# A SwiGLU FFN in two phases: gate and up of the latent tokens as seven half-size products each, the activations kept in DRAM between

## The chip, the core and the metric

One core of one Trainium2 chip runs the whole program. The metric is the device time of one execution in microseconds (us); the kernel before was run three times, and the median counts. Engines are named as the profile names them: PE (TensorE, matmuls; PEld is its weight load), DVE (VectorE), ACT (ScalarE), POOL (GpSimd) and SP (SyncE, whose queue issues the DMAs).

## The reference, cut to what matters

Two layers. Each has a token mixer and then an FFN on 1280 tokens of 1024 channels: 256 context tokens and 1024 latent ones. The mixer ends in a dense output projection `w_out`. The FFN of a layer is

```python
def _swiglu(h, w_gate, w_up, w_down):
    return (jax.nn.silu(h @ w_gate) * (h @ w_up)) @ w_down

FFN_HIDDEN = -(-8 * D_MODEL // (3 * 256)) * 256      # 2816
```

on `h`, the residual stream after an RMS norm, a gain and a shift. Its result is normalised and added to the residual stream. All inputs and weights are float32.

## The kernel before, in words

**Layout.** Activations are channel-major, `[128, 8 channel tiles, tokens]`, and the tokens form three blocks `BLK`: block 0 is the 256 context tokens, blocks 1 and 2 are 512 latent tokens each. Layer 1 is the last one and drops the context (only blocks 1 and 2 go through its FFN).

**Precision.** Every dense product is three matmuls in float32r. A weight is split into a rounded part and the rest: a cast on ACT (`whi`, line 433) and a subtraction on POOL (`wlo`, line 434), in `weights`. An activation is split the same way into `xh` and `xl`. `dense_cm` (line 440) then runs, for each of eight tiles of 128 input channels, whi.xh, whi.xl and wlo.xh into one PSUM bank: 24 matmuls for 128 output channels of one block.

**The FFN** (`out_ffn`, line 1455) runs passes over the blocks: block 1, then blocks 0 and 2 together (layer 0), or block 1, then block 2 (layer 1). A pass goes through 11 pairs `pr` of hidden tiles of 128. For each hidden tile of the pair it loads and splits the 128 columns of gate and of up, runs `dense_cm` for both, takes the silu from exponentials and a logarithm (`silu`, line 727), multiplies (line 1490), and splits the product into `hh` (ACT, line 1491) and `hl` (DVE, line 1492). Then, in the same iteration, it multiplies with the pair's rows of `w_down`, split into `dh` (ACT, line 1502) and `dl` (POOL, line 1503), and adds the result on DVE (line 1517) into `facc`, or copies it there on ACT for the first pair (line 1515). So a pair costs one block 96 matmuls for gate and up and 48 for down, and nothing of the hidden activations leaves the chip.

**Around it.** `w_out` (line 1441) projects the mixers' outputs, which `y_load` (line 1428) reads back from DRAM (`yt`) and splits; blocks 1 and 0 are projected while the GLA mixer, the last of the three, still runs, block 2 after it. `mid` in `run` is `resid` (line 388: RMS norm of the projection, gain, add to the residual stream loaded from DRAM, store) followed by `split_norm` (line 374: the second norm, into `xh` and `xl`). `rstd` (line 345) is the sum of squares: ACT squares, DVE and POOL add (lines 366, 368). `out_ffn` emits two of block 2's eight output tiles of `w_out`, then `mid(1)`, the other six, `mid(0)` and `mid(2)`, and then the passes.

**What sets the order.** The Tile framework orders each engine's instructions when the program is built: it takes the order in which the code emits them as priority, and lets a later instruction that its own simulated timeline shows ready go ahead. At run time every queue is in order, SP's too. PSUM is eight banks of 512 float32 a partition: three for `pd` (gate, up, projections), three for `pm` (down), two for `pn` (norms).

## Time and profile before

| | us |
|---|---|
| median of three runs (4211.9 to 4219.88) | 4216.71 |
| the profiled execution, span from first to last instruction | 4221.6 |
| PE busy in it | 3927.3 |
| the stretch of layer 0's FFN | about 1240 to 2250 |
| the stretch of layer 1's FFN, to the end | 3377 to 4222 |

The profiled execution has no time of its own beside its span; the span lies 4.9 us above the median of the runs. A matmul's duration in a row is longer than the step from one matmul to the next, because matmuls are pipelined: the step is read from start to start. A group of rows gives the count, the busy time, the mean duration of one in nanoseconds, and the idle time before them with what ended it. Some matmul records are missing from the trace, so counts of matmuls are taken from the code.

### The profile page before, as it was taken

Reading aid. Unit: us, or ns where it says so; the run is one execution under the profiler, and the core shown is the slowest. Engines: PE = TensorE matmul, PEld = TensorE weight load, DVE = VectorE, ACT = ScalarE, POOL = GpSimd, SP = SyncE. Lnnn points to the kernel's source line nnn. Section 1 sums busy time; section 2 is a strip of 40 time slices with the busy share of each in tenths; the row PEclk is TensorE's granted clock in tenths of the full one; section 3 lists DMA queues with packets and bytes.
Section 4 is the critical chain, followed back from the end, with each engine's and each line's share of the span. In section 5 each row is a group of like instructions: output and inputs, shape, how many; then the busy total and the mean of one; then the engine's idle time right before and its main releaser. Section 6 shows DMA issues by size and latency. Waiting matters only on the chain. (4 is left out here: it accounts for less than half of the span.)

```text
span 4221.6 us, 74050 instructions
## 1 busy us (share of the span) xinstructions
PE 3927.3 (93%) x29094; PEld 3157.3 (75%) x29094; DVE 2346.4 (56%) x4053; ACT 1629.1 (39%) x3267; POOL 1730.6 (41%) x1686
## 2 busy tenths in 40 slices
PE   7998999899999999999998997999888979999998
PEld 3776888776677788888885675887856757888886
DVE  4565656658756633644445464666658565335444
ACT  4442334234435333522224443343244344334332
POOL 3155630323456544522223145640423465445443
PEclk8998999899999999999998998999989989999999
DMA  6586545665433333322222387554764253334332
GB/s 191 129 235 183 140 125 146 191 186 184 126 120 112 108 92 106 97 65 60 61 60 92 86 225 202 129 148 135 206 196 122 66 157 96 99 94 134 93 97 93
DMA packets 822655, 547.18 MB, mean 130 GB/s; under 512 B 317853, under 2 KB 727201, under 8 KB 822305
## 3 DMA queue, kind: packets, MB, share of 16 engines
q1 hardware_dynamic: 822016, 541.38, 44.9%
q8 instruction: 229, 3.75, 0.4%
q14 instruction: 122, 0.99, 0.1%
q0 software_dynamic: 288, 1.05, 0.1%
HBM read 421.96 MB, written 120.33 MB: 128 GB/s over the span
## 5 line engine op out<-in xcount | busy, mean ns | idle before, releaser
L243 PE MATMUL pd<-xh,whi 128*128 128x512 f32 (+1 forms) x2608 | 981.8, 377 | 30.8 <-ACT whi L433 13.9
L434 POOL TENSOR_TENSOR wlo<-wraw,whi 128x1024 fp32r<-128x1024 f32 (+1 forms) x328 | 678.4, 2072 | 786.8 <-ACT whi L433 652.2
L243 PE MATMUL pd<-xl,whi 128*128 128x512 f32 (+1 forms) x2608 | 987.7, 379 | 12.4 <-DVE xl L1437 4.6
L243 PE MATMUL pd<-xh,wlo 128*128 128x512 f32 (+1 forms) x2608 | 982.5, 377 | 15.7 <-POOL wlo L434 15.7
L243 PEld LDWEIGHTS pd<-xh,whi 128*128 128x128 f32 x2608 | 500.3, 192 | 135.1 <-DVE xh L384 18.8
L243 PEld LDWEIGHTS pd<-xl,whi 128*128 128x128 f32 x2608 | 500.5, 192 | 122.9 <-issue 13.4
L243 PEld LDWEIGHTS pd<-xh,wlo 128*128 128x128 f32 x2608 | 500.6, 192 | 118.3 <-POOL wlo L434 20.5
L433 ACT CAST whi<-wraw 128x1024 fp32r<-128x1024 f32 (+1 forms) x328 | 289.2, 891 | 483.1 <-PE pd L243 266.9
L1517 DVE TENSOR_TENSOR f<-pm,f 128x512 f32<-128x512 f32 (+1 forms) x400 | 247.2, 635 | 354.1 <-PE pm L243 354.1
L1503 POOL TENSOR_TENSOR dl<-draw,dh 128x512 fp32r<-128x512 f32 x176 | 242.6, 1378 | 480.2 <-ACT dh L1502 450.8
L243 PE MATMUL pm<-hl,dh 128*128 128x512 f32 (+1 forms) x880 | 327.6, 373 | 8.1 <-DVE hl L1492 8.1
L243 PE MATMUL pm<-hh,dh 128*128 128x512 f32 (+1 forms) x880 | 322.3, 374 | 9.4 <-DVE f L1517 3.9
L243 PE MATMUL pd<-whi,xh 128*128 128x256 f32 x1072 | 317.6, 297 | 1.9 <-DVE st L438 1.9
L243 PE MATMUL pm<-hh,dl 128*128 128x512 f32 (+1 forms) x880 | 318.2, 372 | 0.0
L243 PE MATMUL pd<-wlo,xh 128*128 128x256 f32 x1072 | 317.8, 297 | 0.0
L243 PE MATMUL pd<-whi,xl 128*128 128x256 f32 x1072 | 317.7, 297 | 0.0
L1502 ACT CAST dh<-draw 128x512 fp32r<-128x512 f32 x176 | 109.1, 620 | 456.7 <-DMA draw<-in_w_ffn_down 245.1
L236 ACT ACTIVATE silu<-silu 128x512 f32<-128x512 f32 (+2 forms) x332 | 171.7, 517 | 191.9 <-DVE silu L731 185.7
L243 PEld LDWEIGHTS pd<-whi,xh 128*128 128x128 f32 x1072 | 213.2, 199 | 8.9 <-issue 3.2
L243 PEld LDWEIGHTS pd<-wlo,xh 128*128 128x128 f32 x1072 | 214.1, 200 | 7.1 <-issue 5.4
L243 PEld LDWEIGHTS pd<-whi,xl 128*128 128x128 f32 x1072 | 213.5, 199 | 7.2 <-issue 5.0
L1492 DVE TENSOR_TENSOR hl<-sg,hh 128x512 fp32r<-128x512 f32 (+1 forms) x110 | 179.5, 1632 | 57.1 <-ACT hh L1491 57.1
(296 smaller groups left out, 7161.2 us busy)
## 6 DMA issues: line engine op xcount, KB each, us to landing
wmod<-in_w_mod SPq DMA_DIRECT2D x192, 256.0 KB
draw<-in_w_ffn_down SPq DMA_DIRECT2D x176, 256.0 KB
wraw<-in_w_ffn_gate SPq DMA_DIRECT2D x88, 512.0 KB
wraw<-in_w_ffn_up SPq DMA_DIRECT2D x88, 512.0 KB
wraw<-in_w_in SPq DMA_DIRECT2D x100, 256.0 KB
a<-ops SPq DMA_DIRECT2D x80, 288.0 KB
X<-ops SPq DMA_DIRECT2D x36, 480.0 KB
wraw<-in_w_out SPq DMA_DIRECT2D x32, 512.0 KB
```

Source lines behind the costliest of these rows:

```text
L236: i = self.nc.scalar.activation(out, in_, f, bias=bias, scale=scale)
L243: return self.nc.tensor.matmul(out, l, r, start=start, stop=stop)
L433: nc.scalar.copy(wh[i][:, :, w], r)
L434: nc.gpsimd.tensor_tensor(wl[i][:, :, w], r, wh[i][:, :, w].bitcast(F32), op=ALU.subtract)
L1492: nc.vector.tensor_tensor(hl[q][b], sg, hh[q][b].bitcast(F32), op=ALU.subtract)
L1502: nc.scalar.copy(dh[:, w], raw)
L1503: nc.gpsimd.tensor_tensor(dl[:, w], raw, dh[:, w].bitcast(F32), op=ALU.subtract)
L1517: nc.vector.tensor_tensor(facc[b][:, m, :], ps[:, :n], facc[b][:, m, :], op=ALU.add)
```

## The change

The FFN becomes `ffn`, in two phases.

**Phase 1** makes the hidden activations and stores them in DRAM (`self.H`). For latent tokens the 2x2 block form of the product, two halves of the 1024 input channels by two hidden tiles by two halves of the tokens, takes seven products of half size in place of eight (`quad`; Strassen's scheme in Winograd's variant). The sums of activations are made once for each layer (`operands`, `operands_late`), the sums of weights for every quad on DVE (`diff`), and the sums of products when PSUM is read. Two of the products accumulate onto a bank that has been read (`first=False`). Layer 0 takes block 1 and block 2 as the two halves (512 columns a matmul) and does the context block alone before that, with plain products (`hidden_plain`). Layer 1 halves each block (256 columns a matmul): the first two pairs (`J1`) for block 1 alone, pairs 2 to 10 for both blocks with shared weights, then the first two for block 2. `gate` takes the silu of a whole pair at once.

**Phase 2** loads the activations again, splits them (`hh`, `hl`) and does the down product, in the passes of before.

Beside that: gate, up, down and output weights are laid out by the host so that one load is `[128, 2048]` with a partition's 8 KB in one run; they are split in pieces of 512 columns (`slot`, four in flight); `w_out` yields after two output tiles instead of one. `pd` has four banks in the FFN and `pn` one. The norms' scratch `nv` has two buffers instead of four. The second norm is made in place (`norm_here`) before the operands, and the residual loads go to a pool of their own (`XO`). Pools for norms, projections and FFN move to other places in SBUF; between the layers the PSUM pools are closed and opened again. The mixers are as before.

The core of the diff (the removed `out_ffn` and `w_out` are in the listing above; `res`, `norm` are `resid`, `norm_here` of block b; what follows the down product is as before):

```diff
-NV = 4
+NV = 2
...
+NS = 4
+J1 = 2
...
+        self.H = [self.t(self.dram, [128, HT, TOK], f"h{i}") for i in range(2)]
...
+    def norm_here(self, x, b, A, B, s):
+        n = BLK[b][1]
+        rs = self.t(self.N, [128, 512], "nrs", bufs=1)[:, :n]
+        self.rstd(x, b, rs)
+        for kt in range(KT):
+            (self.nc.gpsimd if kt % 3 == 2 else self.nc.vector).tensor_tensor(x[:, kt, :], x[:, kt, :], rs, op=ALU.mult)
+            self.act(x[:, kt, :], x[:, kt, :], AF.Identity, bias=B[:, kt, s:s + 1], scale=A[:, kt, s:s + 1])
+    def resid(self, f, b, gp, s, xsrc, xdst, pe=False, px=None):
-        xo = self.t(self.A2 if b == 2 else self.A01, [128, KT, n], f"xl{b}")
...
         self.dma(xo, xsrc[:, :, t0:t0 + n])
         rs = self.t(self.N, [128, 512], "nrs", bufs=1)[:, :n]
...
+    def raw(self, p, src):
+        r = self.t(p, [128, 2048], "raw", bufs=2)
+        self.dma(r, src)
+        return r
+    def slot(self, p, src, e):
+        hi = self.t(p, [128, 512], "shi", F32R, bufs=NS)
+        lo = self.t(p, [128, 512], "slo", F32R, bufs=NS)
+        self.nc.scalar.copy(hi, src)
+        e.tensor_tensor(lo, src, hi.bitcast(F32), op=ALU.subtract)
+        return hi, lo
+    def mm3(self, ps, w, c0, xh, xl, start, stop, skip=False):
+        a, c = w[0][:, c0:c0 + 128], w[1][:, c0:c0 + 128]
+        self.mm(ps, a, xh, start, False, skip)
+        self.mm(ps, a, xl, False, False, skip)
+        self.mm(ps, c, xh, False, stop, skip)
+    def w_out(self, l, p, bs, f, bank, py):
+        y = {b: self.y_load(l, b, f[b], py) for b in bs}
+        for m2 in range(KT // 2):
+            raw = self.raw(p, self.I["wo"][l, m2])
+            for m in range(2):
+                w = [self.slot(p, raw[:, 1024 * m + 512 * k:1024 * m + 512 * k + 512], self.nc.gpsimd) for k in range(2)]
+                for b in bs:
+                    ps = bank()[:, :BLK[b][1]]
+                    for kt in range(KT):
+                        self.mm3(ps, w[kt // 4], 128 * (kt % 4), y[b][0][:, kt, :], y[b][1][:, kt, :], kt == 0, kt == KT - 1)
+                    self.nc.scalar.copy(f[b][:, 2 * m2 + m, :], ps)
             yield
...
+    PRODUCTS = ("11", "S2", "S3", "S1", "12", "22", "S4")
+    def operands(self, xc, p, T):
+        nc = self.nc
+        v, g = nc.vector, nc.gpsimd
+        n = xc["11"][0].shape[2]
+        def split(name, kt, src, e):
+            h, lo = xc[name]
+            nc.scalar.copy(h[:, kt, :], src)
+            e.tensor_tensor(lo[:, kt, :], src, h[:, kt, :].bitcast(F32), op=ALU.subtract)
+        for kt in range(4):
+            split("11", kt, T[0][:, kt, :], g if kt % 2 else v)
+        for kt in range(4):
+            a11, a12, a21, a22 = T[0][:, kt, :], T[0][:, kt + 4, :], T[1][:, kt, :], T[1][:, kt + 4, :]
+            s1, s2, s3 = (self.t(self.N, [128, 512], x, bufs=1)[:, :n] for x in ("nsq", "nacc", "nacc2"))
+            v.tensor_tensor(s1, a21, a22, op=ALU.add)
+            v.tensor_tensor(s2, s1, a11, op=ALU.subtract)
+            v.tensor_tensor(s3, a11, a21, op=ALU.subtract)
+            v.tensor_tensor(a21, a12, s2, op=ALU.subtract)
+            for i, (name, src) in enumerate((("S2", s2), ("S3", s3), ("S1", s1), ("12", a12))):
+                split(name, kt, src, g if i % 3 == 2 else v)
+    def operands_late(self, xc, T):
+        for i, name in enumerate(("22", "S4")):
+            h, lo = xc[name]
+            for kt in range(4):
+                x = T[1][:, kt + 4 - 4 * i, :]
+                self.nc.scalar.copy(h[:, kt, :], x)
+                self.nc.vector.tensor_tensor(lo[:, kt, :], x, h[:, kt, :].bitcast(F32), op=ALU.subtract)
+    def xc_tiles(self, p, names, n, i):
+        return {x: tuple(self.t(p, [128, 4, n], f"{x}{k}{i}", F32R) for k in "hl") for x in names}
+    def quad(self, W, S, raw, xcs, out):
+        nc = self.nc
+        v, g = nc.vector, nc.gpsimd
+        ng, n = len(xcs), xcs[0]["11"][0].shape[2]
+        B = raw.rearrange("p (k c x) -> p k c x", k=2, c=2)
+        o = out.rearrange("p c (g t x) -> p c t g x", g=ng, t=2)
+        def diff(a, b):
+            t = self.t(W, [128, 512], "tw", bufs=3)
+            v.tensor_tensor(t, a, b, op=ALU.subtract)
+            return t
+        def prod(bank, name, src, e, first=True):
+            w = self.slot(W, src, e)
+            for i, xc in enumerate(xcs):
+                h, lo = xc[name]
+                for kt in range(4):
+                    self.mm3(bank[:, i * n:i * n + n], w, 128 * kt, h[:, kt, :], lo[:, kt, :],
+                             first and i == 0 and kt == 0, i == ng - 1 and kt == 3, not first)
+        def u(tag):
+            return self.t(S, [128, ng * n], tag, bufs=2)
+        def r(x):
+            return x.rearrange("p (g x) -> p g x", g=ng)
+        pa, pb, pc, pd = (self.pd()[:, :ng * n] for _ in range(4))
+        prod(pa, "11", B[:, 0, 0], g)
+        s1 = u("s1")
+        nc.scalar.copy(s1, pa)
+        t1 = diff(B[:, 0, 1], B[:, 0, 0])
+        t2 = diff(B[:, 1, 1], t1)
+        prod(pb, "S2", t2, v)
+        u2 = u("u2")
+        v.tensor_tensor(u2, pb, s1, op=ALU.add)
+        t3 = diff(B[:, 1, 1], B[:, 0, 1])
+        prod(pc, "S3", t3, v)
+        u3 = u("u3")
+        v.tensor_tensor(u3, pc, u2, op=ALU.add)
+        prod(pd, "S1", t1, v)
+        v.tensor_tensor(o[:, 1, 1], r(pd), r(u3), op=ALU.add)
+        prod(pa, "12", B[:, 1, 0], g, False)
+        nc.scalar.copy(o[:, 0, 0], r(pa))
+        t4 = diff(B[:, 1, 0], t2)
+        prod(pc, "22", t4, v, False)
+        v.tensor_tensor(o[:, 0, 1], r(pc), r(u2), op=ALU.add)
+        prod(pd, "S4", B[:, 1, 1], g, False)
+        v.tensor_tensor(o[:, 1, 0], r(pd), r(u2), op=ALU.add)
+    def gate(self, S, g, n):
+        nc = self.nc
+        e = self.t(S, [128, 2, n], "e")
+        nc.vector.tensor_scalar(e, g, -80.0, None, op0=ALU.max)
+        self.act(e, e, AF.Exp, scale=-1.0)
+        self.act(e, e, AF.Ln, bias="one")
+        self.act(e, e, AF.Exp, scale=-1.0)
...
+    def hidden(self, l, W, S, j, xcs, t0):
+        n = len(xcs) * 2 * xcs[0]["11"][0].shape[2]
+        o = []
+        for i in range(2):
+            raw = self.raw(W, self.I["wgu"][l, j, i])
+            x = self.t(S, [128, 2, n], "gu"[i])
+            self.quad(W, S, raw, xcs, x)
+            if i == 0:
+                self.gate(S, x, n)
+            o.append(x)
+        self.nc.vector.tensor_tensor(o[1], o[1], o[0], op=ALU.mult)
+        self.dma(self.H[l][:, 2 * j:2 * j + 2, t0:t0 + n], o[1])
+    def hidden_plain(self, l, W, S, j, xh, xl, b):
+        nc = self.nc
+        t0, n = BLK[b]
+        g = self.t(S, [128, 2, n], "g0")
+        h = self.t(S, [128, 2, n], "u0")
+        for i in range(2):
+            raw = self.raw(W, self.I["wgu"][l, j, i])
+            for c in range(2):
+                ps = self.pd()[:, :n]
+                for k in range(2):
+                    w = self.slot(W, raw[:, 1024 * k + 512 * c:1024 * k + 512 * c + 512], nc.gpsimd)
+                    for kt in range(4):
+                        self.mm3(ps, w, 128 * kt, xh[:, 4 * k + kt, :], xl[:, 4 * k + kt, :], k == 0 and kt == 0, k == 1 and kt == 3)
+                if i == 0:
+                    nc.scalar.copy(g[:, c, :], ps)
+                else:
+                    nc.vector.tensor_tensor(h[:, c, :], ps, g[:, c, :], op=ALU.mult)
+            if i == 0:
+                self.gate(S, g, n)
+        self.dma(self.H[l][:, 2 * j:2 * j + 2, t0:t0 + n], h)
...
+            for g in gs:
+                g.__exit__(None, None, None)
+        if not last:
+            gXO, XO = self.pool("XO", side=self.a)
+            next(wo)
+            res(0, XO)
+            for _ in wo:
+                pass
+            over(gY)
+            res(1, XO)
+            res(2, XO)
+            over(gXO)
+            gX, X = self.pool("XC", side=self.a)
+            xc = self.xc_tiles(X, self.PRODUCTS[:5], 512, 0)
+            g0, p0 = self.pool("X0", side=self.a)
+            norm(0)
+            xh0, xl0 = (self.t(p0, [128, KT, 256], x, F32R) for x in ("xh0", "xl0"))
+            for kt in range(KT):
+                nc.vector.tensor_copy(xh0[:, kt, :], f[0][:, kt, :])
+                nc.gpsimd.tensor_tensor(xl0[:, kt, :], f[0][:, kt, :], xh0[:, kt, :].bitcast(F32), op=ALU.subtract)
+            T = [f[1], f[2]]
+            for j in range(HT // 2):
+                self.hidden_plain(l, W, p0, j, xh0, xl0, 0)
+                if j == 1:
+                    norm(1)
+                if j == 3:
+                    norm(2)
+                if j == 6:
+                    self.operands(xc, X, T)
+            over(g0)
+            gX1, X1 = self.pool("XC1", side=self.a)
+            xc.update(self.xc_tiles(X1, self.PRODUCTS[5:], 512, 0))
+            self.operands_late(xc, T)
+            over(self.gF2, self.gF01, self.gN)
+            gS, S = self.pool("S", side=self.o)
+            for j in range(HT // 2):
+                self.hidden(l, W, S, j, [xc], 256)
+            over(gS, gX1, gX)
+        else:
+            gX, X = {}, {}
+            xc = []
+            for b in (1, 2):
+                gXO, XO = self.pool("XO", side=self.a)
+                if b == 1:
+                    next(wo)
+                res(b, XO)
+                over(gXO)
+                norm(b)
+                gX[b], X[b] = self.pool("XC", side=self.a)
+                xc.append(self.xc_tiles(X[b], self.PRODUCTS, 256, b))
+                T = [f[b][:, :, 256 * k:256 * k + 256] for k in range(2)]
+                self.operands(xc[-1], X[b], T)
+                self.operands_late(xc[-1], T)
+                if b == 1:
+                    for _ in wo:
+                        pass
+                    over(gY, self.gF01)
+                    gS, S = self.pool("S", side=self.o)
+                    for j in range(J1):
+                        self.hidden(l, W, S, j, xc[:1], 256)
+            over(gS, self.gF2, self.gN)
+            gS, S = self.pool("S", side=self.o)
+            for j in range(J1, HT // 2):
+                self.hidden(l, W, S, j, xc, 256)
+            for j in range(J1):
+                self.hidden(l, W, S, j, xc[1:], 768)
+            over(gS, gX[2], gX[1])
...
+        self.gN, self.N = self.pool("N", side=self.a)
+        for bs in [(1,), (2,) if last else (0, 2)]:
             facc = {b: self.f_tiles(self.F2 if b == 2 else self.F01, [b])[b] for b in bs}
             for pr in range(HT // 2):
+                raw = self.raw(W, I["wd"][l, pr])
                 hh, hl = {}, {}
...
+                    t0, n = BLK[b]
+                    h = self.t(Dp, [128, 2, 512], "h")[:, :, :n]
+                    self.dma(h, self.H[l][:, 2 * pr:2 * pr + 2, t0:t0 + n])
+                    k, bufs = (0, 1) if b == 0 else (1, 2)
+                    hh[b] = self.t(Dp, [128, 2, n], f"hh{k}", F32R, bufs=bufs)
+                    hl[b] = self.t(Dp, [128, 2, n], f"hl{k}", F32R, bufs=bufs)
+                    nc.scalar.copy(hh[b], h)
+                    nc.vector.tensor_tensor(hl[b], h, hh[b].bitcast(F32), op=ALU.subtract)
+                for half in range(2):
+                    w = [self.slot(W, raw[:, 1024 * q + 512 * half:1024 * q + 512 * half + 512], nc.gpsimd) for q in range(2)]
+                    for m4 in range(4):
+                        m = 4 * half + m4
+                        for b in bs:
+                            n = BLK[b][1]
+                            ps = self.pm()[:, :n]
+                            for q in range(2):
+                                self.mm3(ps, w[q], 128 * m4, hh[b][:, q, :], hl[b][:, q, :], q == 0, q == 1)
+                            if pr == 0:
+                                nc.scalar.copy(facc[b][:, m, :], ps)
+                            else:
+                                nc.vector.tensor_tensor(facc[b][:, m, :], ps, facc[b][:, m, :], op=ALU.add)
```

## Rows read from the trace of the kernel before

**Rows 1.** The page's first part: busy time, share of the span, instructions, by engine.

```profile
PE 3927.3 (93%) x29094; PEld 3157.3 (75%) x29094; DVE 2346.4 (56%) x4053; ACT 1629.1 (39%) x3267; POOL 1730.6 (41%) x1686
```

**Rows 2.** Stretches of the two layers' FFNs: busy by engine, granted clock, DMA.

```profile
core 0: us, PE busy (x) PEld busy (x) DVE busy (x) ACT busy (x) POOL busy (x), PEclk, DMA share, GB/s
1300.00:1700.00 400.00, 383.32 (x1637) 307.86 (x1638) 208.23 (x257) 159.95 (x243) 203.97 (x117) 0.98 0.35 106
1700.00:2200.00 500.00, 495.75 (x2835) 432.43 (x2834) 226.79 (x339) 170.35 (x280) 171.73 (x94) 0.99 0.23 68
3377.00:3540.00 163.00, 132.32 (x525) 102.32 (x525) 110.49 (x103) 79.03 (x120) 107.30 (x57) 0.90 0.44 135
3540.00:4180.00 640.00, 639.10 (x2784) 523.10 (x2783) 271.06 (x320) 227.88 (x326) 294.86 (x159) 1.00 0.34 101
4180.00:4222.00 42.00, 22.26 (x80) 14.46 (x78) 18.93 (x25) 9.41 (x15) 6.04 (x4) 0.83 0.30 107
```

**Rows 3.** Chain that ended last, one period of the second layer: start, us, what.

```profile
3588.72 4.59 PE pd L243 x20
...
3621.74 4.59 PE pd L243 x20
```

**Rows 4.** Timeline of ACT, layer 0, second pass: one cast, a period apart.

```profile
2172.95 0.61 ACT L1491 CAST hh<-sg 128x512 fp32r<-128x512 f32 x1
...
2223.04 0.61 ACT L1491 CAST hh<-sg 128x512 fp32r<-128x512 f32 x1
```

**Rows 5.** Timeline of PE: 256-column matmuls back to back, 15 steps apart.

```profile
2174.09 0.28 PE L243 MATMUL pd<-xl,whi 128*128 128x256 f32 x1
...
2175.79 0.28 PE L243 MATMUL pd<-xl,whi 128*128 128x256 f32 x1
```

**Rows 6.** Groups of POOL by shape: count, busy us, mean ns.

```profile
L434 POOL TENSOR_TENSOR wlo<-wraw,whi 128x1024 fp32r<-128x1024 f32 x208 | 509.0, 2448 | 406.1 <-ACT whi L433 297.3 <-PE pd L243 100.5 <-PE pg L243 4.8
L1503 POOL TENSOR_TENSOR dl<-draw,dh 128x512 fp32r<-128x512 f32 x176 | 242.6, 1378 | 480.2 <-ACT dh L1502 450.8 <-PE pd L243 16.2 <-PE pm L243 11.0
...
L386 POOL TENSOR_TENSOR xl<-nv,xh 128x512 fp32r<-128x512 f32 x32 | 47.9, 1503 | 40.1 <-DVE xh L384 40.1
...
L398 POOL TENSOR_TENSOR nv<-f,nrs 128x512 f32<-128x512 f32 x16 | 28.5, 1780 | 40.8 <-ACT nrs L236 23.2 <-DVE f L399 17.6
```

**Rows 7.** Groups of DVE by shape: count, busy us, mean ns.

```profile
L1517 DVE TENSOR_TENSOR f<-pm,f 128x512 f32<-128x512 f32 x320 | 215.3, 689 | 333.7 <-PE pm L243 333.7
L1492 DVE TENSOR_TENSOR hl<-sg,hh 128x512 fp32r<-128x512 f32 x88 | 168.5, 1914 | 47.6 <-ACT hh L1491 47.6
...
L735 DVE TENSOR_TENSOR sg<-pd,silu 128x512 f32<-128x512 f32 x88 | 60.8, 691 | 176.3 <-ACT silu L236 176.2
...
L1492 DVE TENSOR_TENSOR hl<-sg,hh 128x256 fp32r<-128x256 f32 x22 | 11.0, 500 | 9.5 <-ACT hh L1491 9.5
```

**Rows 8.** Timeline of DVE, layer 1: the same subtraction, short and long.

```profile
3399.87 0.68 DVE L1437 TENSOR_TENSOR xl<-f,xh 128x512 fp32r<-128x512 f32 x1
...
3401.13 1.76 DVE L1437 TENSOR_TENSOR xl<-f,xh 128x512 fp32r<-128x512 f32 x1
```

**Rows 9.** Groups of ACT by shape: count, busy us, mean ns.

```profile
L1502 ACT CAST dh<-draw 128x512 fp32r<-128x512 f32 x176 | 109.1, 620 | 456.7 <-DMA draw<-in_w_ffn_down 245.1 <-PE pm L243 211.0
...
L236 ACT ACTIVATE nsq<-f 128x512 f32<-128x512 f32 x81 | 50.9, 628 | 71.8 <-DVE nacc L366 35.2 <-POOL nacc L368 13.6 <-DVE f L1517 9.7
```

**Rows 10.** Timelines of SP and ACT: when layer 1's loads of yt are issued, land.

```profile
3377.65 2.39 SPq L246 DMA_DIRECT2D f<-yt  x3
```

**Rows 11.** Instructions that touch f: copies of block 2's output projection, last start.

```profile
L1449 ACT COPY f<-pd x16: 567/576/585, 1259.5 to 3456.0; 128x512 f32<-128x512 f32 x16
...
3384.38 1.66 ACT L1436 CAST xh<-f 128x512 fp32r<-128x512 f32 x3 [0.32 <-DMA f<-yt]
```

**Rows 12.** Timeline of DVE, layer 1: block 2's residual and norm.

```profile
3468.54 4.79 DVE L398 TENSOR_TENSOR nv<-f,nrs 128x512 f32<-128x512 f32 x3 [0.74 <-ACT nrs L236]
...
3520.91 0.79 DVE L384 CAST xh<-nv 128x512 fp32r<-128x512 f32 x2
```

More of the change, by code (lines that the diff above doesn't have):

```diff
@@ L196, in pd @@
     def pd(self):
-        return self.psd.tile([128, 512], F32, tag="d", name=self.nm("pd"), bufs=3)
+        return self.psd.tile([128, 512], F32, tag="d", name=self.nm("pd"), bufs=self.nd)
     def pm(self):
@@ L202, in pn @@
     def pn(self):
-        return (self.psr if self.banks[2] == NB1 else self.psum).tile([128, 512], F32, tag="n", name=self.nm("pn"), bufs=self.banks[2])
+        return (self.psum if self.banks[1] else self.psr).tile([128, 512], F32, tag="n", name=self.nm("pn"), bufs=self.banks[2])
     def pt(self, tag, bufs):
@@ L240, in act, with mm @@
         return i
-    def mm(self, out, l, r, start=True, stop=True):
-        return self.nc.tensor.matmul(out, l, r, start=start, stop=stop)
+    def mm(self, out, l, r, start=True, stop=True, skip=False):
+        return self.nc.tensor.matmul(out, l, r, start=start, stop=stop, skip_group_check=skip)
     def dma(self, out, in_):
@@ L1439, in y_load @@
         return yh, yl
-    def w_out(self, l, p, bs, f, bank):
-        y = {b: self.y_load(l, b, f[b]) for b in bs}
-        for m in range(KT):
-            w = self.weights(p, [(0, self.I["w_out"][l][:, 128 * m:128 * m + 128])], 128)
-            for b in bs:
-                ps = bank()[:, :BLK[b][1]]
-                self.dense_cm(ps, *w, *y[b])
-                self.nc.scalar.copy(f[b][:, m, :], ps)
+    def raw(self, p, src):
[24 more added lines that the diff above has]
+                    self.nc.scalar.copy(f[b][:, 2 * m2 + m, :], ps)
             yield
@@ L1453, in f_tiles @@
         return {b: self.t(p, [128, KT, BLK[b][1]], f"f{b}") for b in bs}
-    def out_ffn(self, l, passes, f, mid, xh, xl, gp2, A1n, B1n):
-        nc, I = self.nc, self.I
-        self.gF2, self.F2 = self.pool("F2", side=self.a)
-        gW, W = self.pool("W3", side=self.a)
-        last = l == DEPTH - 1
-        f.update(self.f_tiles(self.F2, [2]))
-        wo = self.w_out(l, W, [2], f, self.pd)
-        for _ in range(WM):
-            next(wo)
-        if WM:
-            mid(1)
-        for _ in wo:
-            pass
-        for b in passes[1][::MO]:
-            mid(b)
+    PRODUCTS = ("11", "S2", "S3", "S1", "12", "22", "S4")
@@ new lines, in ffn, with res, norm, over @@
+    def ffn(self, l, f, gp1, A2, B2, gp2, A1n, B1n):
+        nc, I = self.nc, self.I
+        last = l == DEPTH - 1
+        xsrc = self.XD[0] if l else I["xt"]
+        gW, W = self.pool("W", side=self.a)
+        gY, Y = self.pool("Y", side=self.o)
+        wo = self.w_out(l, W, [2], f, self.pd, Y)
+        def res(b, px):
+            self.resid(f[b], b, gp1, 1 if b == 0 else 0, xsrc, self.XD[1], px=px)
+        def norm(b):
+            self.norm_here(f[b], b, A2, B2, 1 if b == 0 else 0)
+        def over(*gs):
+            for g in gs:
[65 more added lines that the diff above has]
+            over(gS, gX[2], gX[1])
+        self.gA01, self.A01 = self.pool("A01", side=self.o)
+        self.gA2, self.A2 = self.pool("A2", side=self.o)
+        self.gF01, self.F01 = self.pool("F01", side=self.a)
+        self.gF2, self.F2 = self.pool("F2", side=self.a)
+        self.gN, self.N = self.pool("N", side=self.a)
+        gD, Dp = self.pool("D", side=self.a)
```

105 lines of the change are left out of this document (34 added, 71 removed).

## The prediction

> **What bounds the kernel now.** I read the page's busy shares first, then the FFNs by stretch, then the chain that ended last for the step of a matmul, then single operations. PE is busy 93% of the span and no other engine over 56% [rows 1]. A matmul's record overlaps the next one's, so the stretches say more: in the settled part of layer 1's FFN PE idles 0.9 of 640 us, in layer 0's 4.3 of 500, at a granted clock of 1.00 and 0.99 [rows 2]. There PE's stream of instructions is the bound, and a matmul that goes is worth its step. At the starts it isn't: PE idles 30.7 of 163 us in layer 1 (clock 0.90) and 16.7 of 400 in layer 0 [rows 2], where projection, residual, norm and split follow one another. The change shortens the settled parts and rebuilds the starts.
>
> **The unit.** A pair of hidden tiles is 144 matmuls of 512 columns for a block. The chain repeats after 33.02 us [rows 3], 0.2293 us each. With the context in the pass, 144 of 256 columns join them and the period is 50.09 us [rows 4]: 17.07/144 = 0.1185 us for 256 columns. Back to back such a step is 0.1133 us [rows 5].
>
> **What the products save.** Layer 0: gate and up of both latent blocks go from 192 to 168 matmuls a pair, 24 x 0.2293 = 5.50 us, in 11 pairs 60.5. Layer 1 halves the columns as well: 192 x 0.2293 = 44.03 us become 336 x 0.1185 = 39.82, in 11 pairs 46.3. At 0.1133 it would be 65.5. I take 0.1185, which a whole pass gave, and keep the other end. The context's gate and up and all down products keep their matmuls; they only move.
>
> **Does a quad stay PE's?** A quad (gate or up of a pair) is 84 x 0.2293 = 19.3 us of PE. POOL has three subtractions at 1.378 us, 4.1 [rows 6]. DVE has five reads of PSUM at 0.69 [rows 7], eight operations with both inputs in SBUF (four weight sums, four subtractions), and its half of gate and last multiplication, six units of 512 columns, four of them with two SBUF inputs. Such an operation takes 0.68 us, or 1.76 [rows 8], and 1.91 on the mean for `hl` at L1492 [rows 7]. With 0.68 DVE needs 13 us a quad; with 1.91 it needs 3.5 + 15.3 + 9.0 = 27.8 and would be the bound. L1492 ran while POOL was busy 294.86 of 640 us [rows 2], mostly in instructions of 2.45 us [rows 6]; in a quad POOL is busy 21% in pieces of 1.38. Scaling the excess of 1.23 us by 21/46 and by 1.38/2.45 gives 0.32: 1.0 us each, 17 us of DVE a quad. So PE leads, by 2.3 us. ACT, with seven casts and two copies at 0.62 and six units of gate at 0.63 [rows 9], has 9.4. PSUM leaves two products or more between a read and the bank's next use, 5.5 us, and four slots of weights three products. So in the settled part I price the new DVE, ACT and POOL work at nothing, hidden under PE; what it costs without that cover is the second rival.
>
> The Trainium skill (SBUF — State Buffer, Who interferes with whom) says that a DVE instruction with two SBUF inputs and a POOL instruction that reads SBUF exclude each other, the later one blocked until the first has ended, and that DVE reading PSUM isn't touched. The trace agrees: 1.91 us at L1492, 0.69 at L735. By the rule such an operation waits for at most one POOL subtraction, on the mean 0.21 x 0.69 = 0.14 us as an estimate, and DVE would need 15 us; the sum stays, the rival gets weaker.
>
> **Layer 0's context stage** is new on its own: 1056 matmuls x 0.1185 = 125.1 us of PE. Its weights used to be shared with block 2 under PE; now POOL splits them for 256 columns alone. POOL: 88 subtractions x 1.378 = 121.3; the context's own 8, half as wide, 6; two norms (each three additions at 1.378 and two multiplications at 1.78), 15.4; six splits of operands at 1.50, 9.0 [rows 6]. That is 152 us: POOL becomes the bound and 27 us are lost. Ends: 0, where PE's 125 cover all, and 62, with every operation at 1.78. Each of its 22 loads is 1 MB through two buffers. In layer 1 the first 1.25 MB of `yt` landed 6.7 us after the issue [rows 10]; with 6 us for 1 MB the buffers turn in (6 + 5.5)/2 = 5.8 us against POOL's 5.5, at worst 6 us in all. In return the 16.7 us of idle in this stretch go, as I count all of its time anew.
>
> **Between the phases** the first loads need pairs stored long ago. Stores of 1 MB a pair have 38 us each; SP waits for the last multiplication of a pair with the next loads queued behind it, but these are two quads ahead. A pair of the down product is 48 x 0.2293 = 11 us of PE; its activations need load, cast and subtraction, some 8 us through one buffer, and are ready. I take 4 us a layer for the switch, 8; ends 0 and 27, if the first load must wait for the last store (6.7 us each way, twice).
>
> **Smaller scratch** (`nv`) lengthens residuals and norms where PE waits: kernel start, between the layers, the tail of 42 us [rows 2]. I take 5 us, ends 0 and 12.
>
> **Layer 1's start.** Block 2's projection ended at 3456.6 [rows 11], its norm and split at 3521.7 [rows 12]: 65 us. That was covered by the first pass of block 1. Now only four quads of block 1 at 256 columns may run, 4 x 84 x 0.1185 = 39.8 us. Behind the projection come residual and norm (65 less some 8 for the split) and then 16 sums and 22 subtractions at 0.50 [rows 7], 19 us: 76 in all. PE idles 36 us, some 6 of which are there now: 30 lost. Ends: 0, if the static order fills the hole with matmuls of block 1, and 55, if DVE, which serves the quads too, falls behind.
>
> **Half quads.** Weights cost DVE as much for 256 columns as for 512: 8 x 1.0 + 5 x 0.42 + 2.5 = 12.6 us against 9.95 of PE. The first four lie in the hole just counted; the four at the end lose 2.7 each, 11; ends 0 and 22.
>
> **Sum** against the profiled 4221.6: 60.5 + 46.3 + 16.7 - 27 - 8 - 5 - 30 - 11 = 42.5 saved, 4179.1; the median lies 4.9 below that execution, so 4174. A difference under 0.2%, 8.4 us, can't be told from no change. About two thirds of what the products and the old idle give is handed back at the edges.
>
> **Rivals.** *First: the edges are covered.* The static order fills the starts, POOL's norms fall into gaps: 60.5 + 46.3 + 16.7 - 8 - 5 = 110.5, 4106 us. For it: POOL and DVE are under half busy in the settled stretch [rows 2]. Against it: the context stage needs POOL for 121 us by count.
>
> *Second, slower: DVE takes PE's place in the quads.* It decides from the point where a two-SBUF operation costs over (19.3 - 3.5 - 1.4)/12 = 1.2 us on the mean. At 1.4, nearly half-way between 1.0 and 1.91, DVE needs 21.7 us, 2.4 more than PE, in 40 full quads 96: 4174 + 96 = 4270. For it: L1492 costs 1.91 now. Against: POOL is busy half as much and in shorter pieces.
>
> *Third: the edges cost their upper part.* Context stage at 1.50 a subtraction, 10 more, and layer 1's start at its end, 25 more: 4209, no change to be seen.
>
> That the products aren't saved isn't a rival: the counts follow from the code.
>
> **Chances.** Forecast 0.52, first 0.13, third 0.15, second 0.20. The forecast's own range, 4140 to 4208, is faster but for 0.02; the third is mostly within 8.4 us of the median (0.10) and else slower (0.05), the second slower. So faster 0.63, same 0.12, slower 0.25. The range 4105 to 4240 takes in the first and third rivals, the forecast with its ends, and leaves out most of the second.
>
> **What would show it.** Right: quads of 19.3 us in layer 0 and 19.9 in layer 1 with PE hardly idle and DVE near 17; a context stage of about 150 us in which PE waits for POOL's subtraction; a hole of about 36 us before layer 1's quads for both blocks, ended by DVE. Wrong: PE waiting inside full quads for DVE's sums or reads (second rival); a context stage at 125 us (first); waits for the loads of activations (the switch); a 256-column step near 0.1133, which gives up to 19 us more.

## The result: slower, and the profile after

The changed kernel takes 4277.28 us (median of 3 runs, 4274.59 to 4278.37) against 4216.71 before: a ratio of 1.0137, 95% interval 1.0118 to 1.0155. The forecast was 4174, faster; the time lies 37 us above its range. The time is near the second rival's 4270, but the rival's mechanism isn't there: in the stretches of full quads below PE is busy 370.00 of 370 us and 350.00 of 350.

The page's first part (answers to [rows 1]), then stretches in the quads of layer 0 and of layer 1 (answer to [rows 2]):

```profile
PE 3871.0 (91%) x30414; PEld 3186.7 (75%) x30414; DVE 2618.5 (61%) x4470; ACT 1738.5 (41%) x3469; POOL 1677.8 (39%) x1780
```

```profile
core 0: us, PE busy (x) PEld busy (x) DVE busy (x) ACT busy (x) POOL busy (x), PEclk, DMA share, GB/s
1530.00:1900.00 370.00, 370.00 (x1634) 306.35 (x1634) 230.36 (x281) 155.80 (x204) 108.66 (x59) 1.00 0.23 85
3600.00:3950.00 350.00, 350.00 (x2919) 350.00 (x2918) 200.15 (x255) 141.63 (x183) 79.31 (x52) 1.00 0.22 79
```

PE is busy 56 us less than before, and still the end comes 55 us later (spans 4276.4 and 4221.6). I cut both traces at the same events: the last store of `yt` in each layer, layer 1's first load of its gates (`glr`), the first weight difference of a quad (`tw`) and the first split of a loaded activation (`hl`). Stretches in us:

| stretch | before | changed |
|---|---|---|
| start to layer 0's last store of `yt` | 1224.9 | 1231.8 |
| from there to layer 1's first `glr` (layer 0's FFN and layer 1's first projections) | 1371.5 | 1429.0 |
| of it: to the first quad / quads / from the first down product | | 269.0 / 425.0 / 735.0 |
| from there to layer 1's last store of `yt` | 780.7 | 769.0 |
| from there to the end (layer 1's FFN) | 844.5 | 846.6 |
| of it: to the first quad / quads / from the first down product | | 44.8 / 523.0 / 278.8 |

Layer 1's FFN came out as forecast, with all but no change: 46.3 - 30 - 11 - 4 - half of the scratch's 5, so 1 us longer, and it is 2 us longer. Layer 0's was to save 44 us (60.5 + 16.7 - 27 - 4 - 2.5) and costs 57.5, so it missed 101. The attention's stretches run the same code in both and differ by 7 and 12 us; the profiled executions of all the kernels below spread over 1227 to 1253 and 765 to 780 there, and no run shows why. So the experiments are read by these stretches, and their whole times only where they settle something.

**Where layer 0 loses.** Its second down pass has two blocks, the context and block 2. First SP's queue, then ACT, then PE, around one pair:

```profile
2128.41 18.27 SPq L249 DMA_DIRECT2D h<-h  x2
2148.70 0.34 SPq L249 DMA_DIRECT2D raw<-in_wd  x1
2152.29 18.27 SPq L249 DMA_DIRECT2D h<-h  x2
```

```profile
2144.95 0.62 ACT L1726 CAST hh<-h 128x512 fp32r<-128x512 f32 x1 [6.56 <-DVE f L1740]
...
2149.96 1.04 ACT L1726 CAST hh<-h 128x1024 fp32r<-128x1024 f32 x1 [3.18 <-DMA h<-h]
```

```profile
2144.62 0.28 PE L246 MATMUL pm<-hh,slo 128*128 128x256 f32 x1
...
2146.93 0.28 PE L246 MATMUL pm<-hh,slo 128*128 128x256 f32 x1
2151.06 1.01 PE L246 MATMUL pm<-hh,shi 128*128 128x512 f32 x2 [3.85 <-ACT hh L1726]
...
2152.93 0.63 PE L246 MATMUL pm<-hh,shi 128*128 128x512 f32 x1
2153.36 0.63 PE L246 MATMUL pm<-hl,shi 128*128 128x512 f32 x1
...
2158.36 0.40 PE L246 MATMUL pm<-hl,shi 128*128 128x512 f32 x1
2158.59 0.39 PE L246 MATMUL pm<-hh,slo 128*128 128x512 f32 x1
```

The stretch behind PE's wait, with its granted clock (the last column but two):

```profile
2151.00:2157.00 6.00, 5.94 (x17) 4.98 (x18) 2.34 (x3) 0.01 (x1) 0.00 (x0) 0.50 0.47 173
```

The second load of a merged SP entry, block 2's, leaves 18 us after the first. It needs the one tile `h`, which holds the context's activations until they are split; their cast (2144.95) waits for the last context matmul of the pair before (2144.62, it ends at 2144.90), since the context's `hh` and `hl` are single. Then come the load, the cast (2149.96) and only then block 2's first matmul. PE waits 3.85 us, and for the 6 us behind the wait its 512-column matmuls follow one another after 0.43 us, not 0.23: the granted clock is 0.50 there, the lower of its two levels. A pair takes 24 us; its matmuls at full rate need 48 x (0.2293 + 0.12) = 16.8.

**Layer 0's start.** PE's waits from 1240 to 1310, from 1310 to 1345 and from 1345 to 1430 (us in all, times, longest):

```profile
PE pd L246 <- ACT yh L1449: 12.8, 1, 12.8
PE pn L246 <- DVE nacc L373: 6.1, 2, 4.6
```

```profile
PE pn L246 <- DVE nacc L373: 17.3, 2, 13.5
PE pd L246 <- DVE xh L1657: 6.4, 1, 6.4
```

```profile
PE pd L246 <- POOL slo L1464: 11.5, 7, 3.1
```

Between the first projections' end (1240.4) and the first context matmul (1335.3) lie 95 us for 44 us of projection; from there to the first quad's matmul (1502.1) 167 us.

### The profile page after: what moved, and what is told of

Read it like the earlier page. It is cut to its first block, busy times and chain, and to the rows that moved or that the text cites. A ratio compares the mean times of both kernels' runs of the same rounds, so it can differ in the third digit from the quotient of the medians.

```text
span 4276.4 us, 78175 instructions
## 1 busy us (share of the span) xinstructions
PE 3871.0 (91%) x30414; PEld 3186.7 (75%) x30414; DVE 2618.5 (61%) x4470; ACT 1738.5 (41%) x3469; POOL 1677.8 (39%) x1780
## 5 line engine op out<-in xcount | busy, mean ns | idle before, releaser
L1464 POOL TENSOR_TENSOR slo<-raw,shi 128x512 fp32r<-128x512 f32 x472 | 693.4, 1485 | 1032.1 <-ACT shi L1463 940.3
L1463 ACT CAST shi<-raw 128x512 fp32r<-128x512 f32 x472 | 288.8, 619 | 522.1 <-PE pd L246 206.4
L246 PE MATMUL pm<-hh,shi 128*128 128x512 f32 (+1 forms) x880 | 342.2, 393 | 52.7 <-ACT hh L1726 49.4
L246 PE MATMUL pm<-hl,shi 128*128 128x512 f32 (+1 forms) x880 | 338.5, 385 | 5.6 <-DVE hl L1727 5.6
L246 PE MATMUL pm<-hh,slo 128*128 128x512 f32 (+1 forms) x880 | 335.3, 381 | 0.0
L246 PE MATMUL pd<-xl,whi 128*128 128x512 f32 (+1 forms) x720 | 279.1, 388 | 12.0 <-POOL xl L390 9.0
L246 PE MATMUL pd<-xh,whi 128*128 128x512 f32 (+1 forms) x720 | 276.0, 384 | 12.7 <-DVE xh L388 12.7
L246 PE MATMUL pd<-xh,wlo 128*128 128x512 f32 (+1 forms) x720 | 273.2, 380 | 1.3 <-POOL wlo L447 1.3
L246 PEld LDWEIGHTS pm<-hl,shi 128*128 128x128 f32 x880 | 175.0, 199 | 40.8 <-DVE hl L1727 9.5
L246 PEld LDWEIGHTS pm<-hh,slo 128*128 128x128 f32 x880 | 174.7, 199 | 30.5
L246 PEld LDWEIGHTS pd<-xl,whi 128*128 128x128 f32 x720 | 142.1, 197 | 51.6 <-POOL xl L390 14.1
```

Source lines behind the costliest of these rows:

```text
L246: return self.nc.tensor.matmul(out, l, r, start=start, stop=stop, skip_group_check=skip)
L1463: self.nc.scalar.copy(hi, src)
L1464: e.tensor_tensor(lo, src, hi.bitcast(F32), op=ALU.subtract)
```

## Experiments

**1. The ring in the down pass.** Three kernels. The swap:

```diff
-        for bs in [(1,), (2,) if last else (0, 2)]:
+        for bs in [(1,), (2,) if last else (2, 0)]:
```

> Layer 0's second down pass takes block 2 before the context, in its loads and in its matmuls; nothing else moves. Theory A (a ring through single buffers): block 2's load can't be issued before the context's split has freed the one tile of activations, and that split waits for the last context matmul of the pair before, since its tiles are single; block 2's split tiles are double, so with block 2 first its load and cast go ahead of time, and the context's are covered by block 2's first matmuls. The pass then goes from 24.0 us a pair to 17 (48 x 0.2293 + 48 x 0.12 = 16.8), 11 x 7.2 = 79 less: about 4198 us, PE's idle in the pass near zero and its clock back at 1.00. Theory B (the pass is paced by its traffic or by the weights' split on POOL): the period stays above 22 us and the time within 20 us of 4277.

And with the residuals and norms in the old order (`for b in sorted(bs)`):

> Block 2 first in the loads and matmuls of layer 0's second down pass, but the context first again in the residuals and norms behind it. Theory A (what the swap alone still lacked lies behind the pass, where PE idled 5.95 us and 15.48 us before the context's norm, which the swap had put last): from the start of layer 0's down products to layer 1's first load of its gates (681 us with the swap, 735 in the changed kernel) takes 660 to 667, the whole 4277 - 54 - 17 = 4206. Theory B (the end of the layer is set by the norms of both blocks on DVE and ACT, in either order): 675 to 685, and 4220.

And the old order with a second tile, nothing else:

```diff
-                    h = self.t(Dp, [128, 2, 512], "h")[:, :, :n]
+                    h = self.t(Dp, [128, 2, 512], "h", bufs=2)[:, :, :n]
```

> The changed kernel with two tiles for the loaded activations of the down pass instead of one; the order is unchanged (context first). Theory A (the ring is closed by that one tile: block 2's load waits for the context's split, that for the last context matmul of the pair before): the loads go ahead, a pair takes about 17.5 us, and from the start of layer 0's down products to layer 1's first load of gates it takes 677 to 685 us, as with the swap, against 735. Theory B (the context's single split tiles alone hold the pass, or its traffic): above 715.

Measured from the first down product to the first `glr`: 681.2 with the swap, 677.9 with the old norms, 672.3 with the second tile, against 735.0. Whole times: 4233.5 (10 runs, 4211 to 4246), 4238.7 (5 runs) and 4209.3 (one run). The whole times hold the attention's spread as well, so the shorter stretch, 677.9, stands beside the longer time. PE's waits in the pass, changed kernel from 2060 to 2350, swap with the old norms in the same window; then one pair of the changed kernel and 69 us of the other:

```profile
PE pm L246 <- ACT hh L1726: 39.3, 10, 6.3
```

```profile
PE pm L246 <- ACT hh L1726: 1.2, 2, 0.9
```

```profile
2147.00:2171.10 24.10, 20.23 (x98) 16.98 (x97) 10.87 (x19) 4.06 (x6) 5.28 (x5) 0.86 0.25 76
```

```profile
2138.00:2207.00 69.00, 67.90 (x379) 57.97 (x378) 41.52 (x72) 15.41 (x24) 21.76 (x16) 1.00 0.31 107
```

Theory A's mechanism holds: one tile more, or another order of the same work, takes 54 to 63 us away. 38 us of that are PE's waits for the cast; the rest fits the half clock behind them (granted 0.86 over the pair, 1.00 in the other kernel). The swap gave less than the 79 that were expected: the pass settles at 17.2 us a pair, but its first pairs are slower and run beside block 1's norm. That the rest lay in the order of the norms was wrong: they gave 3 us, no more than the 4 (731.4 to 735.0) by which kernels with the old pass differ. The second tile came out 5 us below its forecast of 677 to 685, and it shortens layer 1 too: from the first down product to the end 271.7 us against 278.8. PE's waits for the cast there, in the changed kernel from 3985 to 4140 and with the second tile from 3920 to 4075:

```profile
PE pm L246 <- ACT hh L1726: 8.5, 2, 4.6
```

```profile
PE pm L246 <- ACT hh L1726: 4.5, 1, 4.5
```

**2. What the seven products are worth.** Every quad with eight plain products:

```diff
+        for k in range(2):
+            for c in range(2):
+                w = self.slot(W, B[:, k, c], g)
+                for t in range(2):
+                    name = (("11", "12"), ("S1", "22"))[t][k]
...
```

> Every quad computes eight plain products of the same operands and sizes in place of the seven (four weight blocks, each split on POOL and used for two products; no sums of weights, no sums of products; outputs are not the FFN's). Everything else stays, the making of all operands too. Theory A (PE sets the quads, so a product is worth its matmuls): a pair of layer 0 takes 192 x 0.2293 = 44.0 us against 38.1 now, one of layer 1 384 x 0.12 = 46.1 against 40.3: 11 x 5.9 + 11 x 5.8 = 129 more, about 4405. Theory B (DVE's sums hold the quads back, the second rival of the prediction): the plain quads shed 8 of DVE's operations each and lose less than 60 us against now.

4380.99 us, one run, 104 more. By stretches layer 0's start and quads take 754.8 against 694.0, 60.8 more. Layer 0's pairs follow one another after 43.52 us against 38.08, layer 1's after 46.08 against 40.32. So PE does set the quads, and Strassen gives what its matmuls count. Of the 129 expected, 27 are missing in layer 1's FFN (883.5 against 846.6, 37 more for 64): its first two half-width pairs are stored 111 us after the last `yt`, not 141. That fits DVE as the bound of this start, since the plain ones ask less of it; no run separates it.

**3. Layer 0's start, by order alone.** The context's second norm earlier:

```diff
             res(0, XO)
+            norm(0)
             for _ in wo:
...
-            norm(0)
             xh0, xl0 = (self.t(p0, [128, KT, 256], x, F32R) for x in ("xh0", "xl0"))
```

> The context's second norm (in place) is written ahead of the residuals of blocks 1 and 2, nothing else. Theory A (layer 0's start is a chain on DVE: the context's norm comes behind the residuals of the 512-column blocks, PE idle 3.8 + 13.5 + 6.4 us between 1309 and 1335): the context stage starts some 20 us earlier, time 4277 - 20 = 4257, down to 4250 with the clock that the idle costs. Theory B (what follows is set by the latent blocks' norms and operands on POOL and DVE, which end at 1440 whenever the stage starts): the earlier start is given back as waits for POOL's subtractions between 1345 and 1440, time within 8 us of 4277.

The stretch to the first quad went from 269.0 to 259.1, half of theory A's 20 us; the whole, 4269.7 (4 runs), is just inside theory B's 8. The first context matmul comes 25 us earlier (78.2 us behind the last store of `yt`, not 103.5), and the stage takes 15 us longer, so most of the early start is given back. The wait of 13.5 us ahead of the stage went, and one of 6.2 us for the context's first gated product came. The loads of block 2's `yt` by priority:

```diff
+            with self.tc.high_priority(offset=HT_):
+                next(wo)
```

> The loads and splits of block 2's yt (and the first projection step with them) get a high priority in the static order, nothing else. Theory A (PE's idle of 4.6 + 12.8 us between 1240 and 1259 comes from 3 MB of residual loads and 2 MB of weights that stand ahead of block 2's yt in SP's queue): these loads go first, 12 to 17 us less, 4260 to 4265. Theory B (the transfers are only exchanged: the residuals' loads come later and the norms behind them wait): within 8 us of 4277.

Nothing moved, the wait was 12.80 us again and the time 4276.9: the loads need the last store of `yt`, and in SP's queue the residual loads still stood ahead of them. So this kernel doesn't tell the theories apart. The next one does: it keeps the last load of `yt` as `ylast` and orders the two residual loads behind it by a dependency, on top of the earlier norm and the swap with the old norms:

```diff
-        self.dma(xo, xsrc[:, :, t0:t0 + n])
+        d = self.dma(xo, xsrc[:, :, t0:t0 + n])
+        if px and b and xsrc is self.I["xt"]:
+            self.after(d, self.ylast)
```

> As the swap with the context's norm first, and layer 0's start too: the context's second norm ahead of the residuals of blocks 1 and 2, and the 4 MB of these blocks' residual loads put behind block 2's yt in SP's queue by order. Theory A (PE's 12.8 us before block 2's projection is the time of those 4 MB at 0.39 MB a us, 10 us; the norm gives 7 to 10): layer 0's stretch from the first projections' end to the first quad, 265 us in the changed kernel, takes 245 to 249, and the whole is 16 to 20 below the swap with norms. Theory B (DVE and POOL set this stretch with the latent blocks' norms and operands): 255 to 262, and the whole within 8 us of it.

The wait fell from 12.8 to 2.3 us, so the 4 MB were its cause; but the stretch is 268.6, over both theories' ranges and worse than 259.1. PE now waits 11.7 us for casts of weights that are loaded later: the loads only changed places. The whole, 4222.8 us (10 runs), is 16 below the swap with the old norms, as theory A had it, but not by its mechanism: in the two traces the attention's stretches are 8.2 and 9.5 us shorter, and the FFN's are 1.9 longer and 0.2 shorter.

**4. POOL or DVE.** All three kernels have the swap with the old norms and the earlier context norm. In the first, layer 0's context weights are split on DVE:

```diff
-                    w = self.slot(W, raw[:, 1024 * k + 512 * c:1024 * k + 512 * c + 512], nc.gpsimd)
+                    w = self.slot(W, raw[:, 1024 * k + 512 * c:1024 * k + 512 * c + 512], nc.vector)
```

> Layer 0's context stage: the 88 subtractions of weights on DVE instead of POOL. Otherwise as the swap with the context's norm first, and with the context's second norm ahead of the other residuals. Theory A (POOL's and DVE's operations with two SBUF inputs wait for each other, 1.29 us against 1.73 on POOL and 0.68 against 1.76 on DVE, so what is off POOL costs DVE half of POOL's time and shortens DVE's other operations): from layer 0's last store of yt to its first quad, 259 us with POOL, takes 230 to 242. Theory B (DVE, busy 125 us in the stretch, is full): it takes 270 or more.

Every second one, and in layer 1's half quads all on DVE:

```diff
-                    w = self.slot(W, raw[:, 1024 * k + 512 * c:1024 * k + 512 * c + 512], nc.gpsimd)
+                    w = self.slot(W, raw[:, 1024 * k + 512 * c:1024 * k + 512 * c + 512], nc.gpsimd if k else nc.vector)
...
         ng, n = len(xcs), xcs[0]["11"][0].shape[2]
+        if ng * n == 256:
+            g = v
```

> As the kernel with layer 0's context weights on DVE, but there only every second subtraction on DVE, the other on POOL; and in layer 1's half quads all seven subtractions of weights on DVE, none on POOL. Theory A (the two engines exclude each other, so POOL's share is dear): layer 0's stretch to the first quad 242 to 255, between POOL's 259 and DVE's; layer 1 from the first quad to the down products, 526.8 us with three on POOL and 539.7 with seven, 514 to 522. Theory B (DVE is full): layer 0's stretch as POOL's or longer, layer 1's stretch 530 or more.

Both of these all on DVE, with the operands' splits:

```diff
-        v, g = nc.vector, nc.gpsimd
+        v = g = nc.vector
         n = xc["11"][0].shape[2]
```

> As the kernel with layer 0's context weights on DVE, and the operands' splits of both layers and the half quads' subtractions in layer 1 on DVE too. Theory A: layer 0's stretch to the first quad 2 to 8 us below that kernel's, layer 1's from the first quad to the down products 505 to 518, the whole some 40 us below the swap with norms. Theory B (DVE is full): both stretches are longer than with POOL's share.

The stretch to the first quad: 259.1 with POOL, 252.6 shared, 243.6 on DVE, 240.4 with the operands there too. Layer 1's quads: 522.9 to 527.2 in the kernels with three subtractions of a half quad on POOL, 519.8 with none, 516.0 with the operands' splits on DVE. Whole: 4197.4, 4203.8 and 4183.3 us, the last at a ratio of 0.9919 (0.9894 to 0.9944) to before. Groups by shape in the stretch of the changed kernel (1300 to 1505), then of the first of these kernels (1300 to 1480):

```profile
L1464 POOL TENSOR_TENSOR slo<-raw,shi 128x512 fp32r<-128x512 f32 x89 | 128.8, 1474 | 15.6 <-ACT shi L1463 14.3 <-PE pd L246 1.2
...
L398 DVE TENSOR_TENSOR f<-f,nrs 128x512 f32<-128x512 f32 x12 | 18.6, 1613 | 0.0
```

```profile
L1464 DVE TENSOR_TENSOR slo<-raw,shi 128x512 fp32r<-128x512 f32 x85 | 61.3, 732 | 22.5 <-ACT shi L1463 21.9
...
L398 POOL TENSOR_TENSOR f<-f,nrs 128x512 f32<-128x512 f32 x4 | 10.7, 2707 | 14.4 <-ACT nrs L239 14.4
...
L398 DVE TENSOR_TENSOR f<-f,nrs 128x512 f32<-128x512 f32 x12 | 9.6, 863 | 1.0 <-ACT nrs L239 1.0
```

The same subtraction costs 1.47 us of POOL or 0.73 of DVE, and off POOL it frees DVE too: the norm's multiplications, unchanged, fall from 1.61 to 0.86 us (1.68 with the earlier norm alone), while POOL's four of them go from 1.73 to 2.71. All three come out theory A's way, the first 1.6 us above its range of 230 to 242. In layer 0's stage POOL was the fuller engine (busy 152.8 of 166.8 us, DVE 100.7). In layer 1 DVE looked it, 95 of the 100 us before the full quads, and still gained by taking POOL's share.

**5. Layer 1's start.** Without half quads, and with all seven of a half quad's subtractions on POOL, each on top of the swap with old norms:

```diff
-J1 = 2
+J1 = 0
```

> As the swap with the context's norm first, and J1 = 0: layer 1 has no quads of block 1 alone, all 11 pairs are for both blocks. Theory A (DVE is the bound between 3500 and 3600, busy 95 of 100 us, with operands and with half quads that need as much of it as full ones): without the half quads the full ones start some 45 us earlier and last 2 x 40.3 longer, while the 2 pairs of block 2 alone, 42 us, go: about 5 us less to 5 us more. Theory B (the half quads cover PE in a hole that the projection, norm and operands of block 2 set): the full quads start only 10 us earlier, 30 us more in all.

```diff
+        e = g if ng * n == 256 else v
...
-        prod(pb, "S2", t2, v)
+        prod(pb, "S2", t2, e)
```

> As the swap with the context's norm first, and in the half quads of layer 1 (256 columns) all seven subtractions of weights on POOL instead of three there and four on DVE. Theory A (DVE is the bound of layer 1's start): DVE loses 16 subtractions of 0.7 to 1.8 us between 3470 and 3600, the quads for both blocks start 10 to 15 us earlier and the whole is 10 to 15 us less. Theory B (POOL, with 7 x 1.3 = 9.1 us a half quad and the norm's additions, or the two engines' wait for each other, takes DVE's place): within 8 us.

Without half quads the quads take 532.6 and the rest 272.4, with them 526.8 and 279.9: 2 us less in all, inside theory A's 5 and no more than equal code differs by. With POOL's seven the quads take 539.7 and the whole 4252.1 us (4 runs), 13 more in both: neither theory. Groups of DVE around layer 1's start, with seven and with three on POOL (both 3440 to 3610), and with none and the operands' splits on DVE too (3400 to 3580):

```profile
L1539 DVE TENSOR_TENSOR tw<-raw 128x512 f32<-128x512 f32 x14 | 17.2, 1230 | 0.1
```

```profile
L1538 DVE TENSOR_TENSOR tw<-raw 128x512 f32<-128x512 f32 x16 | 14.5, 905 | 0.2
```

```profile
L1540 DVE TENSOR_TENSOR tw<-raw 128x512 f32<-128x512 f32 x17 | 12.7, 747 | 0.2
```

DVE was relieved of four subtractions a half quad and got slower on the weight sums it kept, 1.23 us for 0.905. I had priced only what left DVE, not what POOL's work does to the rest.

**6. Both causes at once.** The second tile for `h`, and the earlier context norm with everything of experiment 4 on DVE:

> The changed kernel with both causes removed: two tiles for loaded activations (order unchanged, context first), and the context's norm ahead of the other residuals with the context's weights, the operands' splits and the half quads' subtractions on DVE. Theory A (the ring and layer 0's start are all that the forecast missed, and they add): stretches as measured apart, 238 to 243 us to layer 0's first quad, 668 to 676 from its down products to layer 1's first load of gates, 513 to 519 for layer 1's quads, 270 to 274 after them; with the attention's 1225 to 1240 and 765 to 780 the whole is 4165 to 4185, where the forecast stood (4174). Theory B (they overlap, or a third cause takes their place): 4195 or more.

4180.5 us (6 runs, 4174.3 to 4183.8), 0.9904 of before (0.9885 to 0.9922). Stretches: 239.4 to the first quad, 669.1 from the down products, 516.4 for layer 1's quads, 272.3 after them. Theory A, with every stretch in its range: the gains add, and this version beats both kernels. Layer 0's FFN now saves 38 us against the kernel before (1333.4 for 1371.5), where the forecast had 44.

## Why the prediction was wrong, and where it was right

**The step that failed most: "Between the phases".** It said of a down pair that its activations "need load, cast and subtraction, some 8 us through one buffer, and are ready". That was worked out for one block. Layer 0's second pass has two, so two loads pass through that buffer in turn, and the split between them needs tiles that the matmuls of the pair before still hold. The price was put at nothing; it measured 63 us (735.0 - 672.3), of some 101 that layer 0 missed, and 7 us in layer 1 (278.8 - 271.7). The prediction's own sign of being wrong, waits for the loads of activations, came, but mostly in the middle of a pass and not at the switch, where it was priced.

**The second: the old idle.** I took 16.7 us as saved, "as I count all of its time anew", and then counted only the context stage: the chain of projection, residual and norms ahead of it, 95 us for 44 of matmuls, had no term. PE idles 42.5 us there. The stage itself was 152 in the forecast and took 167; its bound of 187 held. The stage of the changed kernel, and POOL's longest waits in it:

```profile
1335.30:1502.10 166.80, 143.84 (x1050) 137.37 (x1051) 100.66 (x98) 106.03 (x194) 152.80 (x108) 0.91 0.41 143
```

```profile
POOL slo L1464 <- ACT shi L1463: 9.5, 9, 2.9
```

POOL is the bound, and busy 152.8 us as summed, though its subtraction costs 1.474 us for 1.378. What the sum left out are 14.0 us in which POOL idles, most of them for casts of weights. Of the 38 us that layer 0 missed beside the ring, experiment 6 took 30 back.

**Right:** the saving in layer 0, 60.5 forecast and 60.8 measured. In layer 1 a step of 0.1200 instead of 0.1185 us made it 41 (11 x (44.03 - 40.32)) for 46.3; the back-to-back 0.1133 was not reached. The hole ahead of layer 1's full quads is there, with DVE at its end: PE idles 30.5 us between the end of block 2's projection and 3600, for 36. First that stretch, then its end in two parts:

```profile
3489.30:3600.00 110.70, 80.20 (x446) 69.06 (x446) 105.17 (x162) 62.66 (x127) 50.37 (x36) 0.78 0.21 73
3500.00:3560.00 60.00, 45.75 (x286) 40.55 (x286) 57.44 (x79) 31.23 (x58) 27.91 (x20) 0.86 0.23 79
3560.00:3600.00 40.00, 27.92 (x130) 23.50 (x131) 37.66 (x65) 24.38 (x50) 15.12 (x13) 0.66 0.19 66
```

At the switch itself PE waits 1.6 us in layer 0 and 8.5 in layer 1, for 4 each.

**Luck.** That layer 1's whole was right to 1 us is partly luck. The products gave 5 us less than forecast and the switch took 4 more. But the half quads at the end lost 2 us, not 11: their two pairs are stored 20.36 and 21.74 us behind the pair before, 42.1 for the 39.8 of their matmuls.

**The quads** are PE's by more than forecast. A quad of layer 0 takes 19.04 us and DVE is busy 62% of it, 11.9 us against my 17. Groups of layer 0's quads (1530 to 1900):

```profile
L1464 POOL TENSOR_TENSOR slo<-raw,shi 128x512 fp32r<-128x512 f32 x59 | 108.7, 1842 | 261.1 <-ACT shi L1463 261.1
L1464 DVE TENSOR_TENSOR slo<-tw,shi 128x512 fp32r<-128x512 f32 x77 | 52.7, 684 | 30.3 <-ACT shi L1463 30.3
...
L1538 DVE TENSOR_TENSOR tw<-raw,tw 128x512 f32<-128x512 f32 x38 | 37.2, 979 | 0.7
...
L1598 DVE TENSOR_TENSOR u<-u,g 128x2048 f32<-128x2048 f32 x10 | 22.9, 2288 | 0.0
```

I scaled [rows 7]'s 1.91 us down to 1.0; it is 0.684 for the subtractions, and 0.693 and 0.979 for the two kinds of weight sums. Most of the waiting is on the other side: POOL's subtraction takes 1.842 us here, while DVE runs pieces of up to 2.3 us. The Trainium skill (SBUF — State Buffer, Who interferes with whom) says that the pair of SBUF ports that DVE and POOL share goes to whoever issues first, for a whole instruction, and that this order decides who blocks. Both sides are seen here: POOL is the slow one in the quads, DVE in the context stage. Of the two estimates, the one by that rule, 15 us a quad, was the nearer.

**The rivals.** None of the three was it. The second came out near the measured time by chance, at a place where PE idles 0.0 of 370 us. The third had the context stage longer, and that half of it came (15 us for its 10); its layer 1 didn't. What was missing was a rival with the down pass in it: I had costed each phase with one block at a time.

## What to carry to other kernels

When work is split into phases that pass data through DRAM, follow each staging tile for one whole period with all blocks that share it, and ask which of its readers is released last: a single tile loaded twice a period joins two blocks into one ring. Price PE's idle with the slow matmuls behind it. When both engines are busy at once, try an operation with two SBUF inputs on DVE rather than POOL, even where DVE looks full: here that paid in both layers.

## What the runs showed of the hardware

A wait of 3.85 us cost PE 7 us a pair (24.1 against 17.2 without it): behind it 512-column matmuls stood 0.43 us apart for 6 us at a granted clock of 0.50, and over the pair it was 0.86. Of POOL and DVE, working on SBUF at the same time, either can be the slow one: POOL 1.842 and DVE 0.684 us in one stretch, POOL 1.474 and DVE 1.613 in another. And ten runs of one kernel, the swap, lay between 4211.2 and 4246.5 us, more apart than most single edits here bring; in the traces of the kernels here the largest difference in equal code sits in the attention (layer 0's last store of `yt` between 1227 and 1253 us). The FFN's stretches repeat better: layer 0's quads within 1 us (424.4 to 425.1), layer 1's within 4 (522.9 to 527.2).
